# Moving the output projection's weights, first operand and constants, and one gelu, in a one-layer decoder kernel

## The chip, the cores and the metric

The kernel runs on one core of one Trainium2 chip. The metric is the device time of one execution in microseconds, of which the median over runs is taken. The engines are called by short names: PE is TensorE, the matrix engine, ACT is ScalarE, DVE is VectorE, POOL is GpSimd, and SP is SyncE, whose queue issues most of the transfers. Each engine works through its own queue in order; an instruction that waits holds up all that stand behind it there.

## The reference

One decoder layer is computed on 1024 tokens of width 1024, in float32. Half of the width goes through attention (8 heads of 64, a mixture of three dilated windows), half through an mLSTM (4 heads of 128, in chunks of 128 tokens). Both halves are joined, projected, added to the input and normalised; then every token is routed to 4 of 32 experts.

```python
def _mixer(x, w_in, ...):
    proj = x @ w_in
    qa, ka, va, xm, vm, om, ip, fp = jnp.split(proj, split_at, axis=-1)
    attn = _dilated_attention(...)                     # 8 heads
    hm = _mlstm_chunkwise(qm, km, vm, i_pre, f_pre)    # 4 heads, 8 chunks
    ...
    return jnp.concatenate([attn, hm], axis=-1) @ w_out

def reference(x, ...):
    y = _mixer(h, ...)
    h = _layer_norm(DEEPNORM_ALPHA * h + y, ln1_g, ln1_b)
    y = _moe(h, w_router, ..., w_down, b_down)         # top 4 of 32, clamped SwiGLU
    h = _layer_norm(DEEPNORM_ALPHA * h + y, ln2_g, ln2_b)
```

## The kernel before, in words

Almost every matrix product is computed from float32 operands that are split into a high and a low half (`split`: ACT casts the high half, L111, DVE subtracts it to leave the low half, L112). A product is then three matmuls: high by high, high by low, low by high.

The mixer works through four pairs of heads. For each pair j there are scores in two groups of four row blocks (`scores`, L521 to L530; DVE adds the mask and takes maxima, ACT exponentiates), the products with the values (`values`, L544 to L561: transposes of the probabilities, value products into one bank `pv`, a last transposition L559, and a write to the DRAM buffer `mixd`), two mLSTM chunks (`mlstm`, which write the other half of `mixd`), and the projection for the next pair. In the last pair nothing is left to project.

After that comes the output projection (from L584 on). The eight 128-row pieces of `w_out` are loaded into two buffers `woraw` and split into `woh` and `wol`. Then, for each of eight token tiles t: `mixed(t)` loads the tile of `mixd` (`mixt`, two buffers), transposes it with eight transposes (L663) and splits it into `mh` and `ml`; `project(t, n)` multiplies it with half n of the weights, 24 matmuls of 128x512 (L675), the first half into the PSUM bank `acc`, of which there is one, the second into one of three banks `s`, and DVE adds the scaled input tile `xt` (L677), which frees the bank. `route(t - 1)` transposes the sum z, computes the router's logits without normalising first, and corrects them with the constants `c12`; these constants come from the router's weights and the layer norm's parameters (L612 to L633, with one small matmul, L630). The gates of a tile are transposed (L892) and multiplied with the split down biases `bdh` and `bdl` (L976, L977).

The experts (`experts`) run in a written order of 32 positions. Each position loads its gate, up and down weights in pieces of 512 KB (`raw`, 13 buffers), splits them, and multiplies. `gate_up(i, w, c)` is half c of the gate (w = 0) or up (w = 1) product; `flips` transposes gathered rows (L1114); `act_gate` is the gelu (L1003). In position 0 the gate product accumulates in the banks `acc` and `pv`, and the transposes of the next position's rows go into a pool of PSUM tiles that is laid over them. `prep` finds the rows of an expert two positions ahead: a selection on DVE (L1026), a listing by PE (L1036), and a gather.

The order on each engine is set by a scheduler that places instructions by program order, by priorities (`tc.high_priority`) and by its own estimate of when each is ready; `tc.issue_after(x)` lets what stands under it come only after x in that order. Pools take memory in stack order, so where a pool is opened and released decides what a tile's first write has to wait for.

Of the kernel before, what the change touches and what calls it, by code (L numbers as in the profile page):

```python
# [9 lines left out]
F32 = mybir.dt.float32  # L10
F32R = mybir.dt.float32r
# [11 lines left out]
S = 1024  # L23
D = 1024
NT = S // 128
E = 32
# [79 lines left out]
class Build:  # L106
# [29 lines left out]
    def mixer(self):  # L136
# [396 lines left out]
        def values(j, o, g, P, rl):  # L533
# [24 lines left out]
            for i in range(4):  # L558
# [4 lines left out]
            nc.sync.dma_start(mixd[g * 512:(g + 1) * 512, j * 128:(j + 1) * 128].rearrange("(a p) e -> p a e", p=128),  # L563
                              ao.rearrange("p a h e -> p a (h e)"))

        P0 = scores(o, 0)
        for j in range(4):
            P1 = scores(o, 1)
            mlstm(2 * j)
            values(j, o, 0, *P0)  # L570
            if j < 3:
                qk_proj(j + 1)
            mlstm(2 * j + 1)
            if j < 3:
                o2 = operands(j + 1)
                P0 = scores(o2, 0)
            values(j, o, 1, *P1)
            if j < 3:
                o = o2
        self.pq.release()  # L580
        pa.release()


        pw = tc.alloc_tile_pool(name="pw", bufs=1, side="right", reuse_waits="tile")  # L584
        woh = pw.tile([128, 8, D], F32R, name="woh")
        wol = pw.tile([128, 8, D], F32R, name="wol")
        for k in range(8):
            raw = pw.tile([128, D], F32, name="woraw", bufs=2)
            nc.sync.dma_start(raw, I["w_out"][k * 128:(k + 1) * 128, :])
            self.split(woh[:, k, :], wol[:, k, :], raw)  # L590
        px = tc.alloc_tile_pool(name="px", bufs=1, side="right", reuse_waits="tile")
        pt_.release()
        pm.release()
        po.release()
# [5 lines left out]
        tiles = []  # L600

        def load_tile(t):
            ts_ = slice(t * 128, (t + 1) * 128)
            mx = px.tile([128, D], F32, name="mixt", bufs=2)
            nc.sync.dma_start(mx, mixd[ts_, :])
            xt = px.tile([128, D], F32, name="xt", bufs=2)
            nc.sync.dma_start(xt, I["x"][ts_, :])
            tiles.append((mx, xt))

        load_tile(0)  # L610
        wr = pc.tile([128, 8, E], F32, name="wr")
        nc.sync.dma_start(wr, I["w_router"].rearrange("(k p) e -> p k e", p=128))  # L612
        gbc = pc.tile([128, 2, 8], F32, name="gbc")
        for j, w in enumerate(("ln1_g", "ln1_b")):
            nc.sync.dma_start(gbc[:, j], I[w].rearrange("o (k p) -> p (o k)", p=128))
        br = pc.tile([128, E], F32, name="br")
        nc.sync.dma_start(br, I["b_router"].to_broadcast([128, E]))

        wg = pc.tile([128, 8, E], F32, name="wg")
        nc.vector.tensor_tensor(wg, wr, gbc[:, 0, :, None].to_broadcast([128, 8, E]), op=OP.mult)  # L620
        nc.vector.tensor_tensor(wr, wr, gbc[:, 1, :, None].to_broadcast([128, 8, E]), op=OP.mult)
        cs = pc.tile([128, 2, E], F32, name="cs2")
        for j, w in enumerate((wg, wr)):
            nc.vector.tensor_reduce(cs[:, j], w.rearrange("p k e -> p e k"), axis=AX.X, op=OP.add)
        stack = pc.tile([128, E], F32, name="stack")
        nc.vector.tensor_scalar(stack, C["iota_e"], C["e_col"], None, op0=OP.is_equal)
        of = pc.tile([128, 128], F32, name="of")
        nc.vector.memset(of, 1.0)
        c12p = ps.tile([128, 2, E], F32, name="pv", bufs=1, padded_shape=[128, 16, E])
        nc.tensor.matmul(c12p.rearrange("p a e -> p (a e)"), of, cs.rearrange("p a e -> p (a e)"), start=True, stop=True)  # L630
        c12 = pc.tile([128, 2, E], F32, name="c12")
        nc.vector.tensor_scalar(c12[:, 0], c12p[:, 0], -1.0, None, op0=OP.mult)
        nc.vector.tensor_tensor(c12[:, 1], c12p[:, 1], br, op=OP.add)  # L633
        g1 = pc.tile([128, D], F32, name="g1")
        b1 = pc.tile([128, D], F32, name="b1")
        nc.sync.dma_start(g1, I["ln1_g"].to_broadcast([128, D]))
        nc.sync.dma_start(b1, I["ln1_b"].to_broadcast([128, D]))
        bdr = pc.tile([128, D], F32, name="bdr", tag="bdr")
        nc.gpsimd.memset(bdr[0:32], 0.0)
        for j in range(1, 4):  # L640
            nc.sync.dma_start(bdr[32 * j:32 * j + 32], I["b_down"])
        bdh = self.bdh = self.ph.tile([128, D], F32R, name="bdh")
        bdl = self.bdl = self.ph.tile([128, D], F32R, name="bdl")
        self.split(bdh, bdl, bdr)
        self.route_init()
        self.ais = {}
        zr = pc.tile([128, D], F32, name="zr", tag="zr")
        nc.gpsimd.memset(zr, 0.0)
        nc.sync.dma_start(hs[S:, :], zr)
        nc.sync.dma_start(acc[S:, :], zr)  # L650
        mT, zs = {}, {}
        hl = self.hl = []

        def mixed(t):

            if t:
                load_tile(t)
            mh = px.tile([128, 8, 128], F32R, name="mh", bufs=2)
            ml = px2.tile([128, 8, 128], F32R, name="ml", bufs=2)
            for g in range(2):  # L660
                tp = ps.tile([128, 4, 128], F32, name="s", bufs=N_S)
                for j in range(4):
                    nc.tensor.transpose(tp[:, j], tiles[t][0][:, (4 * g + j) * 128:(4 * g + j + 1) * 128], ident)  # L663
                self.split(mh[:, 4 * g:4 * g + 4], ml[:, 4 * g:4 * g + 4], tp)
            mT[t] = mh, ml

        def project(t, n):
            if n == 0:
                zs[t] = px2.tile([128, D], F32, name="z", bufs=2)
            mh, ml = mT[t]  # L670
            ns = slice(n * 512, (n + 1) * 512)
            a_ = ps.tile([128, 512], F32, name=("acc", "s")[n], bufs=(n_acc, N_S)[n])
            for k in range(8):
                for i, (a, b) in enumerate(((mh, woh), (mh, wol), (ml, woh))):
                    nc.tensor.matmul(a_, a[:, k], b[:, k, ns], start=(k == 0 and i == 0),  # L675
                                     stop=(k == 7 and i == 2))
            nc.vector.scalar_tensor_tensor(zs[t][:, ns], tiles[t][1][:, ns], ALPHA, a_, op0=OP.mult, op1=OP.add)  # L677

        mvs = {}

# [316 lines left out]
    def swiglu_gate(self, pe, kind, src):  # L997
# [187 lines left out]
    def experts(self, pe, ps, rest):  # L1185
# [144 lines left out]
        for i in range(n_pos + 1):  # L1330
# [208 lines left out]
```

## Time and profile before

| | |
|---|---|
| median of 3 runs | 2076.93 us (2076.55 to 2079.40) |
| profiled execution, own time | 2078.55 us |
| its span, first to last instruction | 2076.9 us |
| mean granted clock of PE, share of full | 0.977 |
| PE busy | 1984.8 us (96%) |
| DVE busy | 1531.9 us (74%) |
| ACT busy | 1214.6 us (58%) |

The page gives each engine's busy time over the whole span. A PE at 96% is busy on average; where it stands still, or works at the lower clock, is only seen in stretches. The views used below are: busy time in stretches (with the granted clock), what an engine waited for in a stretch, and the instructions in order of time with the idle time ahead of each and what ended it, in brackets.

### The profile page before, as it was taken

How to read it: one execution, taken by the hardware profiler on the slowest of the kernel's cores; microseconds unless marked ns; L12 is line 12 of the kernel's file. 1: busy time of each engine (PE TensorE's matmuls, PEld its weight loads, DVE VectorE, ACT ScalarE, POOL GpSimd, SP SyncE). 2: the span in 40 equal slices, each digit the busy share in tenths (PEclk: the TensorE clock that was granted, in tenths of full speed). 3: DMA queues.
4: the chain of work that ended last, by engine and by line, in shares of the span. 5: the costliest groups of instructions: out<-in, count | busy, mean ns of one | idle time of the engine just before them, and what ended most of it. 6: DMA issues, size and time to landing. Idle time of an engine off the chain costs nothing.

```text
span 2076.9 us, 33560 instructions
## 1 busy us (share of the span) xinstructions
PE 1984.8 (96%) x11575; PEld 1511.7 (73%) x11575; DVE 1531.9 (74%) x2351; ACT 1214.6 (58%) x1668; POOL 339.6 (16%) x162
## 2 busy tenths in 40 slices
PE   8999999978997999999999999999999999999992
PEld 7987677756775786767777777777777777777771
DVE  4263554565778686877979889798897887987886
ACT  4232554453226465666767677676776776766774
POOL 0000100100002030403303133032130430311100
PEclk9999999988997999999999999999999999999996
DMA  7327466555318687787988989889889898898985
GB/s 236 107 83 180 113 161 156 138 158 188 122 71 332 266 299 259 244 335 259 379 286 340 344 307 366 290 327 348 299 335 336 312 363 292 332 319 292 358 343 183
DMA packets 194782, 543.18 MB, mean 262 GB/s; under 512 B 23964, under 2 KB 60100, under 8 KB 194604
## 3 DMA queue, kind: packets, MB, share of 16 engines
q1 hardware_dynamic: 179760, 493.28, 66.2%
q0 software_dynamic: 13840, 44.57, 8.6%
q10 hardware_dynamic: 1008, 3.15, 0.4%
q8 instruction: 92, 1.51, 0.3%
q14 instruction: 82, 0.67, 0.1%
HBM read 486.10 MB, written 54.82 MB: 260 GB/s over the span
## 4 chain that ended last, share of the span: by engine, by line
PE 66%; DMA 2%; ACT 1%; issue 1%; DVE 1%; SPq 0%; DVEq 0%; POOLq 0%; POOL 0%; ACTq 0%
PE mm L1151 52%; PE fold L1160 8%; PE tr L1114 3%; PE mm L1167 1%; DMA acc<-ym,idx 1%; DMA raw<-in_w_up 1%; PE tr L1036 0%; PE tr L1103 0%; DMA raw<-in_w_gate 0%; ACT fs L1476 0%; ACT fs L1474 0%; DMA fz<-acc 0%; DMA xm<-hs,idx 0%; PE fold L1182 0%; DVE fy L1491 0%
## 5 line engine op out<-in xcount | busy, mean ns | idle before, releaser
L112 DVE TENSOR_TENSOR wlo<-raw,whi 128x1024 fp32r<-128x1024 f32 x768 | 913.9, 1225 | 193.7 <-ACT whi L111 170.9
L111 ACT CAST whi<-raw 128x1024 fp32r<-128x1024 f32 x768 | 805.0, 1052 | 312.6 <-PE mm L1151 268.8
L1151 PE MATMUL mm<-whi,xh 128*128 128x512 f32 x1040 | 336.0, 404 | 0.0
L1151 PE MATMUL mm<-wlo,xh 128*128 128x512 f32 x1040 | 323.0, 392 | 0.0
L1151 PE MATMUL mm<-whi,xl 128*128 128x512 f32 x1040 | 321.8, 391 | 0.0
L1086 POOL DMA_INDIRECT acc<-ym,idx x35 | 69.4, 1982 | 986.6 <-DVE lst L1067 496.5
L1151 PEld LDWEIGHTS mm<-whi,xh 128*128 128x128 f32 x1040 | 186.2, 188 | 59.6 <-issue 23.5
L1151 PEld LDWEIGHTS mm<-wlo,xh 128*128 128x128 f32 x1040 | 195.7, 188 | 42.8
L1151 PEld LDWEIGHTS mm<-whi,xl 128*128 128x128 f32 x1040 | 195.5, 188 | 43.0
L1151 PE MATMUL mm<-whi,hh 128*128 128x512 f32 x528 | 169.6, 402 | 0.7 <-ACT hh L111 0.7
L1151 PE MATMUL mm<-whi,hl 128*128 128x512 f32 x528 | 166.2, 395 | 0.0
L1151 PE MATMUL mm<-wlo,hh 128*128 128x512 f32 x528 | 166.0, 395 | 0.0
L1081 POOL DMA_INDIRECT xm<-hs,idx x35 | 111.3, 3181 | 55.0 <-PE mm L1151 27.9
L1151 PEld LDWEIGHTS mm<-wlo,hh 128*128 128x128 f32 x528 | 99.4, 188 | 23.3
L1151 PEld LDWEIGHTS mm<-whi,hl 128*128 128x128 f32 x528 | 99.2, 188 | 23.2
L1151 PEld LDWEIGHTS mm<-whi,hh 128*128 128x128 f32 x528 | 96.1, 189 | 25.6 <-issue 4.9
L1081 POOL DMA_INDIRECT xf<-hs,idx x12 | 101.4, 8452 | 3.7 <-issue 3.7
L1160 PE MATMUL fold<-raw,xf 128*32 128x256 f32 x1536 | 87.9, 381 | 0.0
L238 PE MATMUL acc<-xh,whi 128*128 128x512 f32 x192 | 78.1, 407 | 0.1
L238 PE MATMUL acc<-xh,wlo 128*128 128x512 f32 x192 | 77.1, 402 | 0.0
L238 PE MATMUL acc<-xl,whi 128*128 128x512 f32 x192 | 76.8, 400 | 0.0
L1160 PEld LDWEIGHTS fold<-raw,xf 128*32 128x32 f32 x1536 | 47.3, 110 | 33.7 <-issue 4.7
(385 smaller groups left out, 2781.7 us busy)
## 6 DMA issues: line engine op xcount, KB each, us to landing
raw<-in_w_down SPq DMA_DIRECT2D x256, 512.0 KB
raw<-in_w_gate SPq DMA_DIRECT2D x252, 512.0 KB
raw<-in_w_up SPq DMA_DIRECT2D x252, 512.0 KB
wraw<-in_w_in SPq DMA_DIRECT2D x24, 256.0 KB
wraw<-in_w_in SPq DMA_DIRECT2D x8, 512.0 KB
aq<-qd SPq DMA_DIRECT2D x8, 512.0 KB
akh<-kd SPq DMA_DIRECT2D x16, 256.0 KB
akl<-kd SPq DMA_DIRECT2D x16, 256.0 KB
```

Source lines behind the costliest of these rows:

```text
L111: self.lasts = self.nc.scalar.copy(hi, src)
L112: self.lastv = self.nc.vector.tensor_tensor(lo, src, hi.bitcast(F32), op=OP.subtract)
L238: nc.tensor.matmul(a_, w, x[:, k, ns], start=(k == 0 and i == 0), stop=(k == 7 and i == 2))
L1081: self.gathered = self.nc.gpsimd.indirect_dma_start(xg, None, self.rows(self.hs, kind), bass.IndirectOffsetOnAxis(ap=idx[:, u:u + 1], axis=0))
L1086: self.nc.gpsimd.indirect_dma_start(self.rows(self.acc, kind), bass.IndirectOffsetOnAxis(ap=idx[:, u:u + 1], axis=0), y, None, compute_op= ...
L1114: self.turned = nc.tensor.transpose(tp[:, j], x[:, (4 * g + j) * 128:(4 * g + j + 1) * 128], ident)
L1151: self.multiplied = nc.tensor.matmul(outs[n], a[:, kk], b[k][:, n * 512:(n + 1) * 512], start=first and kk == 0 and i == 0, stop=kk == 7 a ...
L1160: nc.tensor.matmul(out[m * g:m * g + m], x[:, kk % n, (kk // n) * m:(kk // n) * m + m], raw[:, g * w:(g + 1) * w], start=first and kk == 0 ...
L1167: self.nc.tensor.matmul(outs[n], self.ones[32 * n:32 * n + 3], brow[32 * n:32 * n + 3, w], start=first, stop=False)
```

## The change

The loading and splitting of the output weights (`out_weights`) and the first tile's transposition (`mixed(0)`, at raised priority) are called inside the last pair of heads, between the values of its first group and the last mLSTM chunk, instead of behind it. The input tile `xt` gets its own load (`load_x`), later than before, from another pool. The routing constants become a function that is called behind `project(0, 0)`, only to come after that product's last matmul and after the first operand's last subtraction. In position 0 of the experts the last quarter of the gate and up work, `gate_up(0, 1, 1)`, is to come after the gelu.

```diff
+        def out_weights():
+            nonlocal pw, px, woh, wol
+            pw = tc.alloc_tile_pool(name="pw", bufs=1, side="right", reuse_waits="tile")
+            woh = pw.tile([128, 8, D], F32R, name="woh")
+            wol = pw.tile([128, 8, D], F32R, name="wol")
+            for k in range(8):
+                raw = pw.tile([128, D], F32, name="woraw", bufs=2)
+                nc.sync.dma_start(raw, I["w_out"][k * 128:(k + 1) * 128, :])
+                self.split(woh[:, k, :], wol[:, k, :], raw)
+            px = tc.alloc_tile_pool(name="px", bufs=1, side="right", reuse_waits="tile")
+        def mixed(t):
+            mx = px.tile([128, D], F32, name="mixt", bufs=2)
+            nc.sync.dma_start(mx, mixd[t * 128:(t + 1) * 128, :])
+            mh = px.tile([128, 8, 128], F32R, name="mh", bufs=2)
+            ml = px.tile([128, 8, 128], F32R, name="ml", bufs=2)
+            for g in range(2):
+                tp = ps.tile([128, 4, 128], F32, name="s", bufs=N_S)
+                for j in range(4):
+                    nc.tensor.transpose(tp[:, j], mx[:, (4 * g + j) * 128:(4 * g + j + 1) * 128], ident)
+                self.split(mh[:, 4 * g:4 * g + 4], ml[:, 4 * g:4 * g + 4], tp)
+            mT[t] = mh, ml
...
             if j < 3:
                 qk_proj(j + 1)
+            else:
+                self.pq.release()
+                pa.release()
+                out_weights()
+                with tc.high_priority(PAIR):
+                    mixed(0)
+                split = self.lastv
             mlstm(2 * j + 1)
...
-        load_tile(0)
-        wr = pc.tile([128, 8, E], F32, name="wr")
...
+        def load_x(t):
+            xt = xts[t] = px2.tile([128, D], F32, name="xt", bufs=2)
+            nc.sync.dma_start(xt, I["x"][t * 128:(t + 1) * 128, :])
+        load_x(0)
...
+        def constants():
+            wr = pc.tile([128, 8, E], F32, name="wr")
...
-        mixed(0)
         for t in range(NT):
             project(t, 0)
+            if t == 0:
+                with tc.issue_after(split.ins), tc.issue_after(self.projected.ins):
+                    constants()
             if t + 1 < NT:
                 mixed(t + 1)
+                load_x(t + 1)
...
-            nc.scalar.activation(t[:, o:o + a.shape[-1]], a, AF.Gelu_apprx_sigmoid)
+            self.gelu = nc.scalar.activation(t[:, o:o + a.shape[-1]], a, AF.Gelu_apprx_sigmoid)
...
             if here:
-                gate_up(i, 1, 1)
+                with ExitStack() if i else tc.issue_after(self.gelu.ins):
+                    gate_up(i, 1, 1)
```

How the order moves is shown at three places. The first is SP's queue at the start of the last pair of heads (woraw: a piece of the output weights; xt: a tile of the input; og, wi, xc, nm, va: operands of the last mLSTM chunks); lines with a plus are new, with a minus gone.

```order
 L435 DMA og<-omg 128x512
 L465 DMA wi<-wid 128x4x128
+L576 DMA woraw<-in_w_out 128x1024 x2
 L430 DMA xc<-xcT 128x4x128
 L437 DMA nm<-nmd 128x4x128
-L589 DMA woraw<-in_w_out 128x1024 x2
-L607 DMA xt<-in_x 128x1024 x2
-L589 DMA woraw<-in_w_out 128x1024
+L576 DMA woraw<-in_w_out 128x1024 x2
 L465 DMA wi<-wid 128x4x128
-L589 DMA woraw<-in_w_out 128x1024
 L433 DMA va<-vmd 128x4x128
```

The first two pieces of the weights now go out ahead of xc and nm, the third and fourth together ahead of the last wi, and both loads of xt have left this place.

The second place is PE's queue at the end of the attention. Before (L550: value products, L559: the last transposes, L675: products of the output projection, L630: the constants):

```order
L550 MATMUL pv<-pTs,av 64x256 x2
L550 MATMUL pv<-pTs,av 64x128 x2
L559 MATMUL pT<-cst,os 128x128 x4
L675 MATMUL acc<-woh,ml 128x512
L675 MATMUL acc<-woh,mh 128x512
L675 MATMUL acc<-wol,mh 128x512
L675 MATMUL acc<-woh,ml 128x512
L675 MATMUL acc<-woh,mh 128x512
L675 MATMUL acc<-wol,mh 128x512
L675 MATMUL acc<-woh,ml 128x512
L675 MATMUL acc<-woh,mh 128x512
L630 MATMUL pv<-cs_4458,of 128x64
```

The same place now (L683: products of the projection, L591: the transposes of a mixed tile):

```order
L550 MATMUL pv<-pTs,av 64x256 x2
L550 MATMUL pv<-pTs,av 64x128 x2
L683 MATMUL acc<-wol,mh 128x512
L683 MATMUL acc<-woh,ml 128x512
L683 MATMUL acc<-woh,mh 128x512
L683 MATMUL acc<-wol,mh 128x512
L559 MATMUL pT<-cst,os 128x128 x4
L683 MATMUL acc<-woh,ml 128x512
L591 MATMUL s<-cst,mixt 128x128 x8
L683 MATMUL s<-woh,mh 128x512
L683 MATMUL s<-wol,mh 128x512
```

All but one of the 24 products of the first half now stand ahead of L559, the earlier ones in groups of two to six between the value products; the eight transposes of the first mixed tile have moved up to the last mLSTM chunk; the second mixed tile's transposes and the second half follow L559 at once. The constants' matmul now stands after the twelfth product of the second tile.

The third place is ACT's queue in the first expert position (whi: high halves of weights, sm: the gelu). Before, and then now:

```order
L985 COPY ai<-s 128x512
L111 CAST whi<-raw 128x1024 x12
L1003 ACT_TABLE_LOAD
L1003 ACTIVATE sm<-acc 128x512
L1003 ACTIVATE sm<-pv 128x512
L111 CAST whi<-raw 128x1024 x2
L111 CAST xh<-tr 128x512
```

```order
L996 COPY ai<-s 128x512
L111 CAST whi<-raw 128x1024 x8
L1014 ACT_TABLE_LOAD
L1014 ACTIVATE sm<-acc 128x512
L1014 ACTIVATE sm<-pv 128x512
L111 CAST whi<-raw 128x1024 x6
L111 CAST xh<-tr 128x512
```

The gelu and its table load have moved ahead of the last four of the twelve casts; the queues of PE and DVE are the same as before in this part of the program.

## Rows read from the trace of the kernel before

**Rows 1.** Busy time by stretch (us, busy of each engine, granted PE clock, DMA share).
```profile
488.00:503.00 15.00, 9.97 (x27) 7.35 (x28) 5.52 (x14) 0.12 (x1) 2.61 (x12) 0.54 0.77 212
659.00:674.00 15.00, 9.40 (x40) 7.48 (x38) 9.37 (x10) 11.24 (x13) 0.00 (x0) 0.77 1.03 416
```
**Rows 2.** What PE waited for, 425 to 510 us: total us, times, longest.
```profile
PE s L521 <- DVE mx L525: 5.3, 3, 4.9
PE pv L630 <- DVE cs L624: 3.2, 1, 3.2
PE m L447 <- ACT qT L444: 2.0, 1, 2.0
PE acc L675 <- DVE ml L112: 1.7, 1, 1.7
```
**Rows 3.** The same list from 900 us to the end.
```profile
PE mm L1151 <- ACT hh L111: 0.7, 1, 0.7
```
**Rows 4.** Timeline of ACT: start, us, instruction, idle ahead and its releaser.
```profile
440.77 1.04 ACT L111 CAST woh<-woraw 128x1024 fp32r<-128x1024 f32 x1 [5.09 <-issue]
...
462.54 1.05 ACT L111 CAST woh<-woraw 128x1024 fp32r<-128x1024 f32 x1 [2.70 <-DMA woraw<-in_w_out]
...
475.55 1.05 ACT L111 CAST woh<-woraw 128x1024 fp32r<-128x1024 f32 x1 [0.80 <-DMA woraw<-in_w_out]
```
**Rows 5.** Timeline of SP's queue, 425 to 500 us: issues.
```profile
429.90 2.27 SPq L589 DMA_DIRECT2D woraw<-in_w_out  x2
...
455.78 0.38 SPq L589 DMA_DIRECT2D woraw<-in_w_out  x1
...
461.37 0.38 SPq L563 DMA_DIRECT2D mixd<-ao  x1
...
466.15 0.33 SPq L605 DMA_DIRECT2D mixt<-mixd  x1
...
471.12 0.33 SPq L589 DMA_DIRECT2D woraw<-in_w_out  x1
...
490.15 0.51 SPq L612 DMA_DIRECT2D wr<-in_w_router  x1
```
**Rows 6.** Timeline of POOL, 435 to 440 us: starts that a landing released.
```profile
435.09 1.29 POOL L466 TENSOR_TENSOR wi<-qT,wi 128x512 f32<-128x512 f32 x1 [17.40 <-DMA wi<-wid]
439.43 1.26 POOL L455 TENSOR_TENSOR nm<-nm,cst 128x512 f32<-128x512 f32 x1 [3.05 <-DMA nm<-nmd]
```
**Rows 7.** Timeline of PE, last attention values and first tile of the projection.
```profile
472.01 0.46 PE L472 MATMUL m<-va,w 128*128 128x129 f32 x2 [0.39 <-issue]
...
488.17 0.74 PE L559 MATMUL pT<-cst,os 128*128 128x128 f32 x4 [0.69 <-ACT os L556]
490.59 0.79 PE L675 MATMUL acc<-woh,ml 128*128 128x512 f32 x1 [1.68 <-DVE ml L112]
...
497.55 0.66 PE L630 MATMUL pv<-cs,of 128*128 128x64 f32 x2 [3.18 <-DVE cs L624]
...
503.61 0.48 PE L675 MATMUL s<-woh,mh 128*128 128x512 f32 x1
...
509.18 0.39 PE L675 MATMUL acc<-woh,mh 128*128 128x512 f32 x1
```
**Rows 8.** Timeline of DVE: the down bias's subtraction.
```profile
505.64 1.23 DVE L112 TENSOR_TENSOR bdl<-bdr,bdh 128x1024 fp32r<-128x1024 f32 x1 [0.17 <-ACT bdh L111]
```
**Rows 9.** Timeline of PE, first expert positions.
```profile
664.88 1.12 PE L1114 MATMUL tr<-cst,xm 128*128 128x128 f32 x4 [5.60 <-ACT sm L1003]
...
681.11 0.37 PE L1036 MATMUL tr<-aux,sel 128*128 128x6 bf16 x8
```
**Rows 10.** Timeline of ACT, same place.
```profile
666.58 1.05 ACT L111 CAST whi<-raw 128x1024 fp32r<-128x1024 f32 x1 [0.83 <-DMA raw<-in_w_gate]
```
**Rows 11.** Timeline of DVE, same place.
```profile
672.99 1.29 DVE L1016 TENSOR_SCALAR um<-mm 128x512 f32<-128x512 f32 x2 [1.23 <-PE mm L1151]
...
679.46 1.22 DVE L1026 TENSOR_TENSOR sel<-cst,rkp 128x1024 bf16<-128x1024 f32 x1
```

More of the change, by code (lines that the diff above doesn't have):

```diff
@@ L579, in mixer @@
                 o = o2
[L580 to L591, printed above, removed]
         pt_.release()
@@ L622, in mixer @@
[L622 to L633, printed above, removed]
+        def load_x(t):
+            xt = xts[t] = px2.tile([128, D], F32, name="xt", bufs=2)
+            nc.sync.dma_start(xt, I["x"][t * 128:(t + 1) * 128, :])
+        load_x(0)
@@ L634, in mixer @@
+        stack = pc.tile([128, E], F32, name="stack")
+        c12 = pc.tile([128, 2, E], F32, name="c12")
+        wg = pc.tile([128, 8, E], F32, name="wg")
         g1 = pc.tile([128, D], F32, name="g1")
         b1 = pc.tile([128, D], F32, name="b1")
[L636 to L651, printed above, removed]
-        hl = self.hl = []
[L654 to L665, printed above, removed]
+        def constants():
+            wr = pc.tile([128, 8, E], F32, name="wr")
+            nc.sync.dma_start(wr, I["w_router"].rearrange("(k p) e -> p k e", p=128))
+            gbc = pc.tile([128, 2, 8], F32, name="gbc")
+            for j, w in enumerate(("ln1_g", "ln1_b")):
+                nc.sync.dma_start(gbc[:, j], I[w].rearrange("o (k p) -> p (o k)", p=128))
+            br = pc.tile([128, E], F32, name="br")
+            nc.sync.dma_start(br, I["b_router"].to_broadcast([128, E]))
+            nc.vector.tensor_tensor(wg, wr, gbc[:, 0, :, None].to_broadcast([128, 8, E]), op=OP.mult)
+            nc.vector.tensor_tensor(wr, wr, gbc[:, 1, :, None].to_broadcast([128, 8, E]), op=OP.mult)
+            cs = pc.tile([128, 2, E], F32, name="cs2")
+            for j, w in enumerate((wg, wr)):
+                nc.vector.tensor_reduce(cs[:, j], w.rearrange("p k e -> p e k"), axis=AX.X, op=OP.add)
+            nc.vector.tensor_scalar(stack, C["iota_e"], C["e_col"], None, op0=OP.is_equal)
+            of = pc.tile([128, 128], F32, name="of")
+            nc.vector.memset(of, 1.0)
+            c12p = ps.tile([128, 2, E], F32, name="pv", bufs=1, padded_shape=[128, 16, E])
+            nc.tensor.matmul(c12p.rearrange("p a e -> p (a e)"), of, cs.rearrange("p a e -> p (a e)"), start=True, stop=True)
+            nc.vector.tensor_scalar(c12[:, 0], c12p[:, 0], -1.0, None, op0=OP.mult)
+            nc.vector.tensor_tensor(c12[:, 1], c12p[:, 1], br, op=OP.add)
+            nc.sync.dma_start(g1, I["ln1_g"].to_broadcast([128, D]))
+            nc.sync.dma_start(b1, I["ln1_b"].to_broadcast([128, D]))
+            bdr = pc.tile([128, D], F32, name="bdr", tag="bdr")
+            nc.gpsimd.memset(bdr[0:32], 0.0)
+            for j in range(1, 4):
+                nc.sync.dma_start(bdr[32 * j:32 * j + 32], I["b_down"])
+            bdh = self.bdh = self.ph.tile([128, D], F32R, name="bdh")
+            bdl = self.bdl = self.ph.tile([128, D], F32R, name="bdl")
+            self.split(bdh, bdl, bdr)
+            self.route_init()
+            self.ais = {}
+            zr = pc.tile([128, D], F32, name="zr", tag="zr")
+            nc.gpsimd.memset(zr, 0.0)
+            nc.sync.dma_start(hs[S:, :], zr)
+            nc.sync.dma_start(acc[S:, :], zr)
@@ L674, in project @@
                 for i, (a, b) in enumerate(((mh, woh), (mh, wol), (ml, woh))):
-                    nc.tensor.matmul(a_, a[:, k], b[:, k, ns], start=(k == 0 and i == 0),
-                                     stop=(k == 7 and i == 2))
-            nc.vector.scalar_tensor_tensor(zs[t][:, ns], tiles[t][1][:, ns], ALPHA, a_, op0=OP.mult, op1=OP.add)
+                    self.projected = nc.tensor.matmul(a_, a[:, k], b[:, k, ns], start=(k == 0 and i == 0),
+                                                      stop=(k == 7 and i == 2))
+            nc.vector.scalar_tensor_tensor(zs[t][:, ns], xts[t][:, ns], ALPHA, a_, op0=OP.mult, op1=OP.add)
         mvs = {}
```

18 lines of the change are left out of this document (2 added, 16 removed).

## The prediction

> **What bounds the kernel now.** I read the windows first, then what TensorE (PE) waited for, then the timelines of the places found. From 488 to 503 us PE is busy 9.97 of 15 us at a granted clock of 0.54, so nearly all of it at the lower of its two levels (1.2 instead of 2.4 GHz), and from 659 to 674 us 9.40 of 15 at 0.77 [rows 1]. PE's waits between 425 and 510 us name four places [rows 2]: 4.9 us in the last scores (L521), 2.0 for the query of the last mLSTM chunk (L447), 1.7 for the low half of the first operand (L675) and 3.2 for the routing constants (L630). After 673 us the list of PE's waits is empty up to 900 and shows one of 0.7 us behind that [rows 3], so what is won ahead of 673 should reach the end.
>
> **Output weights earlier in SP's queue.** The 4.9 us begin on ScalarE (ACT): it stands idle 5.09 us before the first cast of an output weight at 440.77 [rows 4], and the last scores' exponentials are queued behind that cast. The profile names no releaser; the load of that weight was issued at 429.90, behind xc and nm and ahead of two loads of x [rows 5]. The wi load of this group was in at 435.09 and nm at 439.43 [rows 6], the weight 1.3 us behind nm. Now the two weight loads are issued ahead of xc and nm, and the x loads are gone. Bounds: the weight lands as before (0 gained; a loss is excluded, since it is issued earlier and 1 MB behind it is gone), or 1.3 us behind wi, at 436.4, and ACT waits 0.7 instead of 5.1 (4.4 gained). I take 4.0, near the second end, because the landings of these rows come in the order of issue. xc and nm land some 2.6 us later; they belong to the last chunk, whose query is only computed behind ACT's cast at 462.54 [rows 4]. By the Trainium skill, "DMA: Bandwidth & Descriptors", section "Queues, rings and completion order", each DMA engine consumes the entries of a queue's ring in order, which would make this term 4.4; an even sharing among the loads would leave it near 1.
>
> The third and fourth weight now stand together, ahead of the wi load that waits for PE. Before, the fourth was issued at 455.78 behind that load [rows 5], and ACT waited 2.70 us for it at 462.54 [rows 4], with the query scaling (qT) next in its queue; that is PE's 2.0 us. The slot of the fourth comes free with the second weight's subtraction, some 4 us before 455.78, which is more than the 2.7. So 2.0 gained (bounds 0 and 2.7).
>
> **First products beside the last attention values.** 23 of the 24 products of the first tile's first half now stand ahead of the last transpose (L559), where there were 2; the sixteen transposes of the first two mixed tiles stand ahead of the second half in both. So I compare at the first product of that half, 503.61 [rows 7], and PE's work up to there is the same. What goes: the 1.7 and the 3.2 us of waits; the 0.69 us ahead of L559 at 488.17, which four products now fill; and the low level. From 490.59 to 503.61 are 13.0 us; without the 3.2 us wait 9.8, for 22 products, one for the constants and four transposes. The next 24 products take 5.57 us (503.61 to 509.18), 0.232 each, so 22 take 5.1, the rest some 0.8, and the low level costs 3.9. Sum: 1.7 + 3.2 + 0.7 + 3.9 = 9.5. If the products ran at the low level between the values too (21 times 0.2 us lost), 5.3 would be left; that is the lower bound. The values' stretch has PE busy almost without a gap, so I keep 9.5.
>
> **New waits.** Four places can give something back.
> The eight transposes of the first operand stand in PE's queue just behind the numerator product that ran at 472.01 [rows 7]; by the 6.0 us above PE reaches them near 466. Everything of the last values is queued behind them. Their load must follow the write of the attention output: write issued at 461.37, load at 466.15, 4.8 us apart [rows 5]; the write moves with the first term to 457.4, the load to 462.2. A load of 512 KB came in 4.4 us after its issue (471.12, cast at 475.55) or 6.8 (455.78, cast at 462.54) [rows 4, 5]. So it lands at 466.6 or 469.0: PE waits 0.6 or 3.0. I take 0.6, the first being the load with other loads around it and no write-then-broadcast ahead. By the Trainium skill, "DMA: Bandwidth & Descriptors", section "Anatomy of one DMA", a DMA costs some 2.0 us plus its bytes at 436 GB/s; an estimate from that puts write and load at 2.6 and 3.2 us, and this wait at 0. The 4.8 us of the row are longer, so the measured one is used.
> The load of x for the first tile is now issued behind the mixed load that waits for the second tile's transposes, some 1.7 us after L559's end. PE needs the accumulator (one buffer) that its addition frees 7.8 us after L559 (17th product, 16 transposes, 24 products). Landing after 4.4 to 6.8 us and 0.7 for the addition give 6.8 to 9.2: 0 to 1.4 of wait. The constants come right behind: from wr's issue at 490.15 [rows 5] to their product at 497.55 [rows 7] passed 7.4 us, so from 2.1 after L559 they are ready at 9.5, and PE comes to them, twelve products on, at 10.6: 0 to 1. Together I take 0.8 (bounds 0 and 3).
> The subtraction for the down bias, 1.23 us on VectorE (DVE) at 505.64 [rows 8], was beside PE's products; now it stands in the gate chain of the first tile, on which PE's next transposition waits: 0.8 (bounds 0 and 1.2).
>
> **Gelu ahead of the casts.** PE waited 5.60 us at 664.88 [rows 9] for the gelu, which stood behind four casts whose weights landed one by one. That wait goes, and the second half of the up product ends near 665 instead of 673. But the same queues hold the next things up. The first half operand of the next expert's gate product is cast behind a weight that lands only at 666.58 [rows 10], so PE starts it near 668. And PE's slot listing, at 681.11 [rows 9], needs the selection on DVE, done at 679.46 + 1.22 = 680.7 [rows 11]. DVE ran from 672.99 to there without a gap; its only reserve is the 1.23 us that it waited for PE at 672.99. So the listing moves to 679.5, 1.6 us earlier, with PE idle some 3 us ahead of it; as after 664.88, the clock will fall, and half of the 23 products behind it then take twice their 0.232 us, 1.9 in all. Net loss 0.3 (bounds: gain 1.6, loss 2.5).
>
> **Sum.** 4.0 + 2.0 + 9.5 - 0.6 - 0.8 - 0.8 - 0.3 = 13.0 us. The profiled execution took 2078.55 us, 1.6 above the median of the three runs shown (2076.93) and within them; 2078.55 - 13.0 = 2065.6, and 2063.9 from the median. I predict 2064.
>
> **Rivals.**
> The first operand comes late. If its load takes as long as the first weight's did, 10.9 us from 429.90 to 440.77, it lands at 473.1: PE waits 7.1 instead of 0.6, and some 2 us more at the low level. 13.0 - 8.5 = 4.5 gained, 2072. For it: everything of the last values is queued behind these transposes. Against: that long load had eight others around it. Chance 0.13.
> The weights land no earlier, because the loads share the bandwidth: the first term is 0 and the second 1, and 8 are gained, 2069. For it: the profile shows no releaser for the 5.09 us. Against: the order of landings. Chance 0.12.
> The gelu does pay: PE runs through to the end of the up product and the selection is not what it meets next. Then 5.6 us and the low level behind it, some 2, come on top: 2056. Against: the listing's place in PE's queue is unchanged. Chance 0.05. In my forecast this part of the change doesn't do what its words say.
> Slower than before, by one mechanism: the load of x and the constants, at SP's end of the line behind a load that itself waits for PE, hold the one accumulator, and PE stands at the second tile at the low level. The wait is the landing time less 5.4 us; with 2 us for the level it eats the gain when x lands 17 us after its issue or later. The longest in this stretch is 10.9 us, which would still leave a gain of about 6 (2071). Chance 0.05, 0.01 of it within what can be told.
> **Numbers.** The forecast case has 0.65, with a range of its own of 2060 to 2069. What a measurement of this kernel can tell from no change is about 0.2%, 4.2 us. Faster by more than that: the forecast, the gelu, the sharing and half of the late operand, 0.65 + 0.05 + 0.12 + 0.06 = 0.88. Within: the rest of the late operand and 0.01 of the last rival, 0.08. Slower: 0.04. The range goes from the gelu's end to the late operand's, 2057 to 2072.
>
> **What would show it.** PE's wait in the last scores under 1.5 us; no wait at the query; the first tile's products spread among the value products at about 0.23 us each; the second half's first product some 14.5 us earlier; PE's clock at the high level between 470 and 500 us; at the first expert no wait for the gelu, but one of about 3 us at the slot listing for DVE's selection. I am wrong if PE stands over 3 us at the transposes of the first operand or at the second tile's first product, or if the gap between the traces shrinks after 673 us.

## The result

| | before | changed |
|---|---|---|
| median of five runs | 2076.60 us (2076.07 to 2079.40) | 2060.11 us (2056.62 to 2066.12) |
| ratio, 95% interval | | 0.9921 [0.9902, 0.9941] |
| profiled execution: own time, span | 2078.55, 2076.9 us | 2062.43, 2060.8 us |
| mean granted clock of PE | 0.977 | 0.983 |

The change saves 16.5 us by the medians; I had predicted 13.0 and a time of 2064. The mechanism was mostly right, three sizes were not, and two of the errors cancel, which is luck.

### The profile after

The same views as before. Busy time by stretch (columns as in [rows 1]):

```profile
488.00:503.00 15.00, 12.38 (x68) 9.33 (x66) 8.88 (x22) 2.82 (x7) 0.00 (x0) 0.89 0.77 239
...
659.00:674.00 15.00, 15.00 (x75) 11.65 (x74) 13.59 (x19) 7.47 (x9) 1.37 (x1) 0.93 1.03 408
```

The stretch from 488 us now has a granted clock of 0.89, where it had 0.54, but PE still stands 2.6 us in it. What PE waited for, 425 to 510 us, answers [rows 2]; the last line is the only one between 640 and 800 us:

```profile
PE m L472 <- issue: 2.9, 2, 2.5
PE acc L683 <- DVE z L685: 2.6, 1, 2.6
PE s L521 <- DVE mx L525: 1.4, 3, 0.9
PE s L591 <- DMA mixt<-mixd: 0.7, 1, 0.7
...
PE tr L1125 <- DVE xl L112: 4.0, 1, 4.0
```

Gone are the query (2.0), the low half of the operand (1.7), the constants (3.2) and the gelu; the 4.9 us in the last scores are 0.9. (The first line stood in the list of before with 2.6.) New are the wait for the sum z at the second tile, a short one for the first mixed tile, and the one for xl at the second expert. The timeline of PE, answering [rows 7] and [rows 9]:

```profile
461.61 0.46 PE L472 MATMUL m<-va,w 128*128 128x129 f32 x2 [0.39 <-issue]
...
462.97 1.09 PE L591 MATMUL s<-cst,mixt 128*128 128x128 f32 x8 [0.68 <-DMA mixt<-mixd]
...
467.20 0.49 PE L683 MATMUL acc<-woh,mh 128*128 128x512 f32 x1
...
482.07 0.60 PE L559 MATMUL pT<-cst,os 128*128 128x128 f32 x4
...
483.53 0.48 PE L683 MATMUL s<-woh,mh 128*128 128x512 f32 x1
...
492.73 0.47 PE L683 MATMUL acc<-woh,mh 128*128 128x512 f32 x1 [2.62 <-DVE z L685]
...
494.42 0.63 PE L683 MATMUL acc<-woh,mh 128*128 128x512 f32 x1
...
497.60 0.39 PE L683 MATMUL acc<-wol,mh 128*128 128x512 f32 x1
...
654.52 1.11 PE L1125 MATMUL tr<-cst,xm 128*128 128x128 f32 x4 [3.96 <-DVE xl L112]
...
665.32 0.37 PE L1047 MATMUL tr<-aux,sel 128*128 128x6 bf16 x8
```

The reader is to see that the first product starts at 467.20, among the values, where before it started at 483.10, that the second half follows the last values at once (483.53 against 503.61), and that PE then stands at the second tile's first product; the row at 494.42 is longer than the one at 497.60, since the clock fell behind that wait and came back.

To compare places without the difference with which two executions begin (the first 425 us, where the orders are equal, took 421.6 to 425.3 us in these runs), I count from the last transposition L559 of the third pair of heads (425.09 us in the trace of before, 424.09 in that of the changed kernel). The numbers are microseconds ahead of before, worked out from the timelines of PE. *Chunk* is the first numerator product of the last mLSTM chunk (472.01 before), *second half* the first tile's second half (503.61), *third tile* its counting product in the routing (L851, 552.48), *listing 1* and *listing 2* the slot listings L1036 at 646.47 and 733.53 (the one at 681.11 [rows 9] lies between them). Behind the last one every kernel took 1342.9 to 1343.7 us to its end.

| kernel | chunk | second half | third tile | listing 1 | listing 2 |
|---|---|---|---|---|---|
| changed | 9.4 | 19.1 | 14.2 | 14.1 | 14.8 |
| e1 gelu back | 7.3 | 16.9 | 14.4 | 14.0 | 13.3 |
| e2 weights only | 9.3 | 7.3 | 7.3 | 6.7 | 7.4 |
| e8 weights and pools | 8.9 | 19.0 | 17.3 | 17.2 | 17.4 |
| e9 pools only | 0.2 | 11.4 | 7.6 | 7.5 | 7.6 |
| e3 x early | 10.1 | 19.4 | 15.8 | 15.4 | 15.6 |
| e4 gb late | 7.8 | 17.4 | 15.8 | 15.2 | 15.9 |
| e5 x early, gb late | 8.4 | 17.6 | 16.3 | 15.5 | 16.6 |
| e6 one operand part first | 8.9 | 18.0 | 16.3 | 16.3 | 16.0 |
| e7 e6, x early, gb late | 9.5 | 18.8 | 17.4 | 17.5 | 16.9 |
| e10 three parts first | 9.1 | 18.4 | 16.3 | 16.5 | 22.5 |
| e11 e10, x early, gb late | 8.0 | 15.4 | 14.1 | 14.2 | 19.9 |
| e12 e10, gelu back | 9.4 | 19.6 | 17.9 | 17.7 | 16.1 |

The rows with the same order up to the second half (changed, e1, e6, e10, e12) spread by 2.1 us at the chunk and by 2.7 at the second half (e1 16.9, e12 19.6), the times of single executions of the changed kernel by 9.5 us, and the five medians of the kernel before by 1.5 (2075.7 to 2077.1); a difference below 2 us between two kernels in one column shows nothing by itself.

### The profile page after: what moved, and what is told of

Read it like the earlier page. It is cut to its first block, busy times and chain, and to the rows that moved or that the text cites. A ratio compares the mean times of both kernels' runs of the same rounds, so it can differ in the third digit from the quotient of the medians.

```text
span 2060.8 us, 33562 instructions
## 1 busy us (share of the span) xinstructions
PE 1978.8 (96%) x11575; PEld 1506.2 (73%) x11575; DVE 1531.8 (74%) x2351; ACT 1214.6 (59%) x1668; POOL 336.0 (16%) x162
## 4 chain that ended last, share of the span: by engine, by line
PE 71%; DVE 3%; DMA 2%; ACT 1%; issue 1%; SPq 0%; DVEq 0%; POOLq 0%; ACTq 0%
PE mm L1162 53%; PE fold L1171 8%; PE tr L1125 3%; PE acc L683 2%; PE mm L1178 1%; PE s L683 1%; DMA acc<-ym,idx 1%; DMA raw<-in_w_gate 0%; PE tr L1047 0%; PE pv L550 0%; PE tr L1114 0%; DMA xt<-in_x 0%; ACT fs L1486 0%; PE pv L743 0%; DMA woraw<-in_w_out 0%
```

## The experiments

Each ran four to eight times beside the kernel before; ratios are to the kernel before.

### The gelu edit undone

```diff
-                with ExitStack() if i else tc.issue_after(self.gelu.ins):
+                if True:
                     gate_up(i, 1, 1)
```

> The changed kernel with one edit undone: the first gelu stands behind the four late casts again; only ScalarE's order differs. Theory, from the two traces: the gap between them was 15.1 us at 647 us and 15.8 us at the slot listing, so this edit was worth 0.7 us, because PE's wait for the gelu is followed or replaced by one for the same landing weights. It then takes 2060.8 us, PE waits 5 to 6 us for the gelu, and no longer 4.0 us for the low half xl at the transposition behind it. My prediction had a loss of 0.3 us: 2059.8. Rival, the gelu edit paid in full: 2067 to 2068. The first two are too close for the time to tell apart; the place of the slot listing tells it, 0.7 us later or 0.3 us earlier than in the changed kernel, measured from the first expert's first listing.

2061.97 us, 0.9934 [0.9919, 0.9949]. PE's wait for the gelu is back:

```profile
648.52 1.12 PE L1125 MATMUL tr<-cst,xm 128*128 128x128 f32 x4 [6.67 <-ACT sm L1014]
```

Between listing 1 and listing 2 it takes 87.8 us, the changed kernel 86.3 and before 87.1. So the gelu edit is worth 0.7 to 1.5 us here, and not the 7.6 of the rival. The size is not told well: the five traces with the gelu behind the casts and nothing else moved there (before, e1, e2, e8, e9) have 86.4 to 87.8 us in this stretch, the four with it ahead (changed, e3, e4, e5) 86.0 to 86.9; the means are 0.7 apart, and the two ranges overlap. A loss of 0.3 is unlikely by that, and not excluded.

### The weights alone

```diff
+            else:
+                self.pq.release()
+                pa.release()
+                pw = tc.alloc_tile_pool(name="pw", ...)
+                for k in range(8):
+                    ...the loads and splits of w_out
             mlstm(2 * j + 1)
```

> The kernel before with one part of the change: the output weights are loaded and split inside the last pair of heads; first operand, input tiles, constants and gelu stay as before. Theory: the two stalls go (4.9 us in the last scores, 2.0 us at the query), and with them the low clock behind each (some 3.4 us), so the first product of the last mLSTM chunk comes 9.4 us earlier than before and the end, if nothing gives it back, at 2067. The prediction's terms without the clock: 6.0 us earlier, 2070.6. Rival, the loads share the bandwidth and the weights land no earlier: 1 us earlier, 2075.6; then most of the gain came from the first products and not from the weights.

2070.47 us, 0.9974 [0.9964, 0.9984]. The last chunk comes 9.3 us earlier, as the theory with the clock has it; ACT's first cast stands as in the changed kernel:

```profile
436.24 1.05 ACT L111 CAST woh<-woraw 128x1024 fp32r<-128x1024 f32 x1 [1.08 <-DMA woraw<-in_w_out]
```

That is 4.0 us earlier than in the kernel before, counted from the third pair's L559, so the weight lands earlier and the rival falls. At the end 7.4 us are left by the trace and 5.2 by the medians, below the 9.4 expected. The first operand and the constants hold PE as before, so nothing is won there:

```profile
483.85 0.50 PE L674 MATMUL acc<-woh,ml 128*128 128x512 f32 x1 [1.67 <-DVE ml L112]
...
490.33 0.41 PE L629 MATMUL pv<-cs,of 128*128 128x64 f32 x2 [3.07 <-DVE cs L623]
```

Another 2.0 us are lost between the chunk and the second half (9.3 to 7.3): PE waits 1.1 us for the first mixed tile, where before it did not, and 3.1 for the copies of the probabilities pTs, where before it was 1.1; a higher clock in that stretch (0.90, before 0.78) gives part of this back.

### Weights and pools; the pools alone

In the diff two buffers change their pools: `ml`, the low half of the operand, goes from `px2` to `px`, `xt` from `px` to `px2`. The next two kernels are both made from the kernel before, the first with the early weights of e2 as well.

```diff
-            xt = px.tile([128, D], F32, name="xt", bufs=2)
+            xt = px2.tile([128, D], F32, name="xt", bufs=2)
...
-            ml = px2.tile([128, 8, 128], F32R, name="ml", bufs=2)
+            ml = px.tile([128, 8, 128], F32R, name="ml", bufs=2)
```

> The kernel before with two edits: the output weights inside the last pair of heads, and two buffers exchanged between the pools, the first operand's low half (ml) into the pool px that is free early and the input tiles xt into px2 that lies over the attention's tiles. The first operand and the constants are called where they were, behind the attention, and the gelu stands behind the casts. PE's order comes out as in the changed kernel but for four transposes. Theory: what moved the first products between the last values, and the constants behind them, was the place of ml in memory, not the place of the calls; the time is that of the changed kernel without its gelu edit, 2061 to 2062, and the second half's first product comes 17 to 19 us earlier than before. Rival: calling the first operand early and the constants late matters for itself; then the time stays near that of the weights alone, 2070.

2060.96 us, 0.9935 [0.9923, 0.9948]: the time of the changed kernel, with `mixed(0)` and the constants called where they were. Its products lie among the values too:

```profile
465.56 0.49 PE L674 MATMUL acc<-woh,mh 128*128 128x512 f32 x1
```

So the exchange of the pools let PE start, and the rival falls. The two buffers were not moved singly, but the first write of `ml` tells which one it was, first in e2, then in e8:

```profile
483.17 0.63 DVE L112 TENSOR_TENSOR ml<-s,mh 128x512 fp32r<-128x512 f32 x1
```

```profile
463.05 0.69 DVE L112 TENSOR_TENSOR ml<-s,mh 128x512 fp32r<-128x512 f32 x1 [0.83 <-ACT mh L111]
```

In e2 the high half `mh` is cast from 465.12 on, and `ml` follows 18 us later; in e8 it follows within 0.7 us of the cast at 462.43. By the code `px2` is opened only when the attention's pools have been released, behind the last values, and `px` ahead of that; `ml` had to wait, as PE did for `ml` [rows 2].

> The kernel before with only ml and xt exchanged between the pools; the output weights are loaded behind the attention as before. It tells how much of the gain the first products bring without the weights. Theory: PE's 4.9 us in the last scores stay, since the first weight is still issued behind xc and nm; of the terms of the first products the waits of 1.7 and 3.2 us and part of the low clock go (6 us), and the wait for the sum at the second tile (1 to 2.6 us) comes instead: 4 us, 2072 to 2073. Rival: without the early weights there is nothing to multiply, and the exchange gains nothing or loses by the late input tile: 2076 to 2079.

2067.74 us, 0.9964 [0.9951, 0.9978]: 8.7 us by the medians and 7.6 by the trace, more than the 4 expected. The scores' wait stays, as expected:

```profile
439.66 0.80 PE L521 MATMUL s<-akh,aq 128*128 128x512 f32 x1 [4.51 <-DVE mx L525]
```

The products need nothing of the early weights: 11.2 us are won between the chunk and the second half. Weights (7.4) and pools (7.6) are two gains that add up to 15.0 of the 17.4 that e8 has with both.

### The wait for the first input tile

> The changed kernel with the first input tile loaded earlier, into a weight buffer that is free by 472 us, instead of behind the attention's last write. Theory: the 2.6 us that PE stood at the second tile, waiting for the sum that frees the accumulator, go, and with them the low clock of the products behind (2.0 us): 4.6 us, 2055.5. Rival: the routing constants, which are issued at the same time as the tile was, hold PE at their product next, since VectorE gets to them only at 493 us: 1 to 2 us gained, 2058 to 2059. If the wait was no loss at all: 2060.

```diff
-            xt = xts[t] = px2.tile([128, D], F32, name="xt", bufs=2)
+            xt = xts[t] = (px2 if t else pw).tile([128, D], F32, name="xt" if t else "woraw", bufs=2)
...
                     mixed(0)
+                load_x(0)
```

2060.11 us, 0.9924 [0.9912, 0.9936], no change that the time can tell. PE's wait at the second tile is gone, but it stands twelve products later, at the constants' product, as the rival had it:

```profile
491.85 0.41 PE L653 MATMUL pv<-cs,of 128*128 128x64 f32 x2 [1.75 <-DVE ln_mv L694]
```

> The changed kernel with two loads of 512 KB (the last layer norm's parameters, first used at 2033 us) issued some 90 us later instead of just ahead of the attention's last write and the first input tile; PE's order differs by the place of one small product. It tells why that tile took 6.8 us to land. Theory: 1 MB stood ahead of it in the transfers; without it the tile lands after about 4.4 us, PE waits under 0.5 us at the second tile, the clock stays up, and 4 us are gained: 2056. Rival: the tile is late for its place behind a write and a read of the same buffer, not for the bandwidth: it still takes over 6 us, and the time stays within 1 us of 2060.

```diff
-                nc.sync.dma_start(self.gb[:, 0], I["ln2_g"].to_broadcast([128, D]))
-                nc.sync.dma_start(self.gb[:, 1], I["ln2_b"].to_broadcast([128, D]))
+                with tc.issue_after(self.xload4.ins):
+                    ...the same two loads (xload4: the load of the fifth input tile)
```

2059.06 us, 0.9918 [0.9905, 0.9931]. Here are the issues and the sum that waits for the tile, first in the changed kernel, then with the two loads away:

```profile
481.15 0.33 SPq L1354 DMA_DIRECT2D gb<-in_ln_g  x1
481.53 1.43 SPq L1355 DMA_DIRECT2D gb<-in_ln_b  x1
...
485.04 0.49 SPq L626 DMA_DIRECT2D xt<-in_x  x1
...
491.89 0.69 DVE L685 SCALAR_TENSOR_TENSOR z<-xt,acc 128x512 f32<-128x512 f32 x1 [6.32 <-DMA xt<-in_x]
```

```profile
487.34 0.44 SPq L626 DMA_DIRECT2D xt<-in_x  x1
...
492.43 0.69 DVE L687 SCALAR_TENSOR_TENSOR z<-xt,acc 128x512 f32<-128x512 f32 x1 [3.97 <-DMA xt<-in_x]
```

The tile takes 5.1 us instead of 6.9, so 1 MB ahead of it cost 1.8 us; PE's wait falls from 2.6 to 0.2. The time does not show it. Between the second half and the third tile the changed kernel's trace gives back 4.9 us, this one 1.6, but e1, e6, e8, e10 and e12, with the tile issued at the same place as in the changed kernel, only 1.7 to 2.5, with a wait of 0.9 to 1.7 us for the sum: the profiled execution of the changed kernel is the worst of these. (Three kernels have both edits: e5 and e7 below, and e11.)

> Both late-layer edits together: the first input tile early in a free weight buffer, and the last layer norm's parameters out of the way. Each alone took PE's 2.6 us wait at the second tile away, but with the tile early PE then stood 1.7 us for the routing constants' product, which came behind the same 1 MB. Theory: with both there is neither wait, and from the second half's first product to the third tile's route pass 49.5 to 50.5 us (53.8 in the changed kernel, 52.5 and 50.5 with one edit); 3 us are won, 2057. Rival: the constants stay late for their place in the queue behind the attention's last write; then nothing beyond either edit alone, 2059.

2059.28 us, 0.9913 [0.9900, 0.9927]. The third tile is 1.3 us behind the second half's lead, so from one to the other pass 50.1 us, as the theory had it, but the gain in the time, expected at 3, is 0.8 and not told from none.

### What stands behind the gelu

> The changed kernel with the chain behind the gelu shortened: the second expert's first half operand is split (xh, xl) ahead of that expert's weights on ScalarE and VectorE, and the third expert's slot selection is computed before the up product. Theory: the gelu edit paid only 1.4 us of 7.6 because PE met these two next (it stood 4.0 us for xl); with both ahead, that wait falls under 1.5 us, the listing comes 2 to 4 us earlier, and the time is 2057. Rival: the landing of the second expert's gate weights, one per 2.5 us, bounds the place; PE then waits as long for the weights' low halves, the first product of that expert starts no earlier than 656.1 on the changed kernel's clock, and the time stays 2060.

```diff
             do(tx, 1)
+            if i == 0:
+                xs, xv = self.lasts, self.lastv
...
+            if i == 1:
+                with tc.issue_after(xs.ins), tc.issue_after(xv.ins):
+                    gate_up(i, 0, 0)
```

(Besides, the selection is computed ahead of `gate_up(0, 1, 0)`.) 2059.60 us, 0.9922 [0.9908, 0.9935]. Only the first of four operand parts was ahead of the weights, and PE's wait moved to the next:

```profile
655.62 1.12 PE L1125 MATMUL tr<-cst,xm 128*128 128x128 f32 x4 [4.71 <-DVE xl L112]
```

On ACT that part's cast stood at 654.26, behind six weights of the same expert, cast as they landed. That does not tell queue order from landing; a kernel further below, e10, does, with `xs` and `xv` set behind `do(tx, 2)` and so three parts ahead. First e6 and e5 together:

> The edits of the two kernels above together, on the changed kernel. If each theory holds, the gains add: 6 us, 2054. If the weights' landing bounds the first experts, what is won ahead of them is lost there (as 0.7 us were between 640 and 665 us when the gelu edit was undone), and the time is 2057 to 2060.

2061.03 us, 0.9921 [0.9908, 0.9935]: no gain, as the rival had it, though e10 shows that its reason, the landing, is not the right one. PE waits 4.6 us for xl here too.

> The changed kernel as with the operand put first, but now three of the four operand parts of the second expert are split ahead of its weights (with only the first ahead, PE's 4.0 us wait became one of 4.7 us for the next). Theory: the place is bound by the order of ScalarE's and VectorE's queues; PE's waits between 640 and 670 us fall to under 2 us in all, and from the first expert's first listing to the second listing pass 3 us less than the changed kernel's 86.3 us (2060.8 less 1343.1 is 717.7, less 631.4). Time 2057. Rival: the weights land too slowly (the transfers run at 410 GB/s there, one 512 KB piece per 1.3 to 2.5 us), PE waits for weights instead and the stretch stays within 1 us of 86.3; 2060.

2055.41 us (2054.90 to 2059.00), 0.9908 [0.9893, 0.9923]. PE's waits between 640 and 670 us, and the casts of the operand, now ahead of the weights:

```profile
648.08 0.73 PE L1162 MATMUL mm<-wlo,xh 128*128 128x512 f32 x2 [0.34 <-DVE wlo L112]
...
651.11 0.66 PE L1125 MATMUL tr<-cst,xm 128*128 128x128 f32 x4 [0.32 <-DVE xl L112]
...
654.04 0.73 PE L1162 MATMUL mm<-wlo,xh 128*128 128x512 f32 x2 [0.73 <-DVE wlo L112]
```

```profile
649.74 1.07 ACT L111 CAST xh<-tr 128x512 fp32r<-128x512 f32 x2 [2.50 <-PE tr L1125]
650.70 2.01 ACT L111 CAST whi<-raw 128x1024 fp32r<-128x1024 f32 x2
```

From listing 1 to listing 2 pass 81.1 us instead of 86.3. The transfers ran at the same rate (the last column is GB/s; first the changed kernel, then this one):

```profile
640.00:659.00 19.00, 15.04 (x64) 11.60 (x63) 14.55 (x15) 10.98 (x14) 1.10 (x2) 0.88 1.02 410
```

```profile
640.00:655.00 15.00, 13.56 (x73) 9.91 (x72) 13.15 (x17) 8.89 (x12) 1.10 (x2) 1.00 1.02 409
```

So it was the queues' order and not the landing, and the rival falls. Against e6 (87.4 us in this stretch) only the number of parts differs; both compute the selection early, so how much of the 5.2 us needs that too is not shown.

> The operand parts ahead of the weights (three of four, which took 5.2 us out of the first experts' stretch and ran in 2055.4), and with them the first input tile early and the last layer norm's parameters late. Theory: the two places are independent, and the 1.7 us that the trace showed for the tile and the parameters come on top: 2053.7. Rival: what is won at the second tile is lost at the first experts' weights, whose transfers run at 410 GB/s: 2055 to 2056.

2056.32 us, 0.9900 [0.9887, 0.9914]. The stretch takes 81.4 us again; nothing is seen of the other two edits, nearer to the rival.

> The operand parts ahead of the weights, with the gelu edit undone: the gelu stands behind the four late casts again. Theory: the gelu edit was worth little in the changed kernel because the operands' chain ended next; with that chain out of the way it is worth the whole wait for the gelu, 5 to 7 us, so this takes 2061 to 2062, PE waits 5 to 7 us for the gelu, and the stretch from the first expert's first listing to the second takes 86 to 88 us instead of 81.1. Rival: the operands' place alone gave the 5.2 us, and the gelu is worth 1 to 2 us here too: 2057.

2061.00 us, 0.9928 [0.9914, 0.9942].

```profile
644.60 1.11 PE L1125 MATMUL tr<-cst,xm 128*128 128x128 f32 x4 [6.07 <-ACT sm L1014]
```

88.7 us between the listings against 81.1: with the operand out of the way the gelu edit is worth 7.6 us by the trace, 5.6 by the medians and 4.2 by the two ratios, about the theory's size. Alone the gelu edit gives at most 1.5 (e1 against the changed kernel), and the operand's place nothing (88.7 in e12 against 87.8 in e1). The kernel e10 is the fastest run; its interval overlaps that of the changed kernel, but e11 and the listings say the same.

## Why the prediction was right, and where it was wrong

**The weights' place: the waits right, the clock left out.** Two terms, 4.0 and 2.0. The waits measured just that: 4.9 to 0.9, and 2.0 to 0. ACT now casts the first and fourth weight so:

```profile
435.78 1.05 ACT L111 CAST woh<-woraw 128x1024 fp32r<-128x1024 f32 x1 [1.10 <-DMA woraw<-in_w_out]
...
453.04 1.05 ACT L111 CAST woh<-woraw 128x1024 fp32r<-128x1024 f32 x1
```

The first comes 1.35 us behind the start that wi's landing released (434.43; forecast 1.3). By the Trainium skill, "DMA: Bandwidth & Descriptors", section "Queues, rings and completion order", each engine consumes a ring's entries in order; the trace agrees, with the weight now in ahead of nm (439.93). But the chunk came 9.4 us earlier (7.3 to 10.1 in the runs that load them so), not 6.0. Most of the difference is PE's low level behind each wait, which the timeline of before shows:

```profile
443.52 0.80 PE L521 MATMUL s<-akh,aq 128*128 128x512 f32 x1 [4.88 <-DVE mx L525]
444.12 0.63 PE L523 MATMUL s<-akl,aq 128*128 128x512 f32 x1
444.54 0.63 PE L521 MATMUL s<-akh,aq 128*128 128x512 f32 x1
444.97 0.63 PE L523 MATMUL s<-akl,aq 128*128 128x512 f32 x1
...
460.80 1.16 PE L442 MATMUL m<-xc,wq 128*128 128x128 f32 x8
...
464.46 1.88 PE L447 MATMUL m<-xc,wk 128*128 128x128 f32 x8 [1.96 <-ACT qT L444]
```

From 444.12 on the products stand 0.43 us apart, and eight 128x128 products take 1.88 us behind the wait at the query, 1.16 ahead of it. I had priced that level for the first products and for the gelu, and forgot it here. This is the largest error, 3.4 us by this trace.

**First products beside the values: right in size, for a reason I did not name.** 9.5 less 0.6 at the operand's transposes make 8.9; the lead grew by 9.7 between the chunk and the second half (9.0 to 10.2 in the others with early weights and exchanged pools, but 7.4 in e11). PE waits 0.68 us at L591, forecast 0.6: the write was issued at 454.69, the load at 459.21, and PE had it at 462.97. That the two agree is partly luck: the load went out 3.0 us ahead of the forecast and took 0.6 less, and PE came 3.7 us ahead of its own. The second half came 20.1 us earlier, of which 1.0 belongs to the start; I had said 14.5. But I took the new order as it stood and did not ask what made it possible. e8 shows that it is the pool in which `ml` lies and not the place of the calls.

**The input tile and the constants: too cheap in this execution.** 0.8 (0 to 3), and 0.8 for the down bias. From the second half to the third tile the changed kernel gives back 4.9 us: 2.6 of wait, 1.4 for the low level that follows (seven products from 493.99 to 496.98 stand 0.43 us apart, where 0.23 is the high level), 0.3 for the constants' product, and 0.6 that I can't place. The tile took 6.9 us to land, beyond the 6.8 I had as the far end, for the 1 MB of another layer ahead of it, which I saw in SP's queue of before and did not count. The down bias cost nothing that shows: PE waits 0.2 us at the gates. In the other kernels' executions 1.7 to 2.5 us are given back, near the 1.6.

**The gelu: the sign of a small term wrong, the mechanism one step off.** I had PE wait some 3 us at the listing for the selection. It waited 4.0 us one step earlier, for xl, in the same queues. I had named that step, the half operand cast behind a weight that lands late [rows 10], and put no wait of PE there:

```profile
651.56 1.04 ACT L111 CAST whi<-raw 128x1024 fp32r<-128x1024 f32 x1 [1.45 <-DMA raw<-in_w_gate]
652.51 0.58 ACT L111 CAST xh<-tr 128x512 fp32r<-128x512 f32 x1
```

```profile
653.78 0.69 DVE L112 TENSOR_TENSOR xl<-tr,xh 128x512 fp32r<-128x512 f32 x1
```

The clock fell there, as I said, and 0.7 us were gained where I had 0.3 lost. The 0.3 has a slip in it: half of the 23 products at 0.232 us more each are 2.7 us, not 1.9, so my own terms make a loss of 1.1. That the edit "doesn't do what its words say" held; e12 shows why, and that its price was real.

**The sum.** From the trace: 9.4 + 9.7 - 4.9 + 0.6 = 14.8 at listing 2. The rest of the 16.1 us between the two spans is the start (1.0) and 0.3 behind it. Without the start that makes 15.1, and 18.0 with the more usual 2 us given back; the medians' 16.5 lies between. That the sum of 13.0 came so near is partly luck: 3.4 us too little at the weights and 3.3 too little given back cancel. Of the rivals, none came, and the gap between the traces did not shrink after 673 us. Of the signs, the second half's place, the listing's wait and the clock failed: from 470 to 500 us the clock was 0.94, at the low level from 493.99 to about 497.3. Left open: why executions with the same order spread by 2 to 3 us between 425 and 485 us.

## What to carry to other kernels

Price a wait of PE together with the low clock that follows it, every time: here 6.0 us of stalls less brought 9.4. When a product cannot start early, look at which pool its operand's memory lies over before moving the calls. When a wait is removed, go on down the queues of the engines behind it until the next instruction that lands or is cast late; of two edits here, one paid 1.5 us at most alone and the other nothing, and both together 6.7 (87.8 us in e1, 81.1 in e10).

## What was not expected of the hardware

Behind the wait of 2.62 us at 490.11 the first five products still stood 0.23 to 0.31 us apart (492.73 to 493.99); only then did PE fall to 0.43 us, until the constants' product at 496.98. So the price of a wait can stand in rows a little behind it. And in e4 a load of 512 KB still took 5.1 us from its issue to its first use, with one load of its size and a write of 256 KB issued within 1 us ahead of it; by the Trainium skill, "DMA: Bandwidth & Descriptors", section "Anatomy of one DMA", whose figures are fitted on the path through GpSimd, a fixed 2.0 us and the bytes at 436 GB/s make an estimate of 3.2, 4.4 with the other load ahead and 5.0 with the write too. The prediction's estimate by that section left out which path it is for; these loads are issued by SP, and from the write's issue to that of the load that reads it the trace has 4.5 us, where that estimate has 2.6. The rate was far from 436 GB/s here: around this load in e4 the DMA engines were busy 0.96 and 0.99 of the time and moved 247 and 235 GB/s (last two columns; the tile's issue and first use are shown above), against 409 at the first experts. Why is open.

```profile
487.00:490.00 3.00, 3.00 (x15) 2.47 (x14) 1.46 (x4) 0.34 (x1) 0.12 (x1) 1.00 0.96 247
490.00:493.00 3.00, 3.00 (x18) 2.38 (x16) 0.57 (x1) 0.37 (x1) 0.00 (x0) 1.00 0.99 235
```
